# One layer of a hybrid attention trunk: memory queries and outputs on scaled float16, part of the ff1 row sums inside the MLP loop, and another order of the splits

## Chip, core and metric

The kernel runs on one core of one Trainium2 chip. The core has a matrix engine (TensorE, PE in the profile), VectorE (DVE), ScalarE (ACT), GpSimd (POOL) and the engine that issues most transfers (SyncE, SP). The metric is the device time of one execution in microseconds; 1422.9 us is the median of three runs of the kernel before (1422.52 to 1423.31).

## The reference

x is 1024 rows of 1024 numbers; everything is float32. One layer (the two attentions themselves are left out):

```python
h = rmsnorm(x, g_mix_pre)
proj = h @ w_in                     # q, k, v of 8 + 8 heads of 64, 8 forget logits
y = concat(rmsnorm(fox_attention, g_fox_out), rmsnorm(chunked_attention, g_chk_out))
x = x + rmsnorm(y @ w_out, g_mix_post)
h = rmsnorm(x, g_mem_pre)
mem_n = rmsnorm(mem, g_mem_kv)      # 256 memory rows
q = h @ w_mq                        # 4 heads of 256
p = softmax(q @ (mem_n @ w_mk).T / 16)
y = (p @ (mem_n @ w_mv)) @ w_mo
x = x + rmsnorm(y, g_mem_post)
h = rmsnorm(x, g_ff_pre)
y = square(relu(h @ w_ff1)) @ w_ff2 # 1024 -> 4096 -> 1024
x = x + rmsnorm(y, g_ff_post)
```

## The kernel before

Every float32 product is made of three matmuls on a high and a low part of each operand (`mm3`, L202 to L206: high*high, low*high, high*low; in the profile L204, L205, L206). The parts are either a rounded 32-bit form, or float16 after a scaling by a power of two that keeps them in range. Before the change, queries, keys, values of the first attention and the MLP are on scaled float16; the memory block is on the 32-bit form. A split is always ACT (copy or scaled copy to the high part) and then DVE or POOL (rest minus high part to the low part).

The program has three pieces. First the entry: norm of x, transposes, values. Then attention in eight pairs of heads, with the k and v of the memory behind it. Then a second phase: output projection (tiles `yw`), norm and transposes (`tr_h2T`), memory queries (`mq`, a Strassen product of seven half-size products), scores (`ms`), transposes of the probabilities (`mtr`), memory outputs (`mo`), and the output projection of the memory (`ym`, Strassen for rows 0 to 511, plain for the others). Last the MLP: a loop over j = 0 to 15, each a Strassen step on one 128-column block of each of the two halves of w_ff1 (products on PE in the order `px`, `py`, `px`, `pz`, `px`, `pv`, `pz`), then the second product (`fx`). The rows of w_ff1 that are meant by "rows" below are its 32 column blocks of 128.

Attention and second phase are ordered by a planner that runs when the program is built (`Flow`, L58). PE's work comes as streams of steps, each with a cost and a condition; the first stream whose condition holds gives the next step. Work of the other engines goes into queues for V (DVE), S (ACT), G (POOL) and D (transfers) by `put`, with an earliest time, a cost and a level; when an engine is free the item of the lowest level that is due is issued (`upto`, L95). `Tokens` (L41) count buffers. `Stock` (L413) loads and splits the weights in a fixed list; `Norms` (L1249) loads w_ff1 once more during attention, block by block, for the sums of squares (`wn`) from which the scale of all of w_ff1 is made (`sw1`, its inverse `us1`; both columns of `fsc`). `close_row` (L1411) ends a row block of a projection: root of the sum of squares, addition to x, store, square sum of the new x, root, scaling.

The MLP's order is written by hand. In iteration j, `nxt` is the block of j + 1 and `after` that of j + 2. `Weights` (L2577) holds the two raw slabs of a block (`wf`), their Strassen sums made by POOL (`sc`, `sd`, L2595 to L2602), and the splits: `whi_a`, `wlo_a` of the first slab, `v0hi_s` and so on of the sums. `nxt.split("a")` stands between the fourth and the fifth product of an iteration; the first two products of the next iteration read it. `relu2` (L2360) applies the inverse scale and squares. `first_row` (L2397) makes the first two products. Iterations up to `AHEAD` = 7 have part of their work done earlier. At j = 14 `second_scales` (L1315) makes the scale of w_ff2 and of the squared features.

## Time and profile before

| | |
|---|---|
| median of 3 runs | 1422.9 us |
| profiled execution | 1422.69 us |
| its span | 1420.7 us |
| granted PE clock over the span | 0.999 |
| busy: PE, DVE, ACT, POOL | 98%, 81%, 69%, 32% |

The span is from the first to the last instruction of the core; about 2 us of the device time lie outside it. A matmul's record is longer than its pitch, since consecutive matmuls overlap; where PE is gapless its time is the number of matmuls times the distance of their starts. Views are quoted as they print: a timeline row has start, duration, engine, line, operation, and in brackets the idle time before it and what ended that; a group's row has busy time, mean duration in ns, and the idle time before its members.

### The profile page before, as it was taken

What the parts mean: (1) busy time and instruction counts of PE and PEld (TensorE: products, weight loads), DVE (VectorE), ACT (ScalarE), POOL (GpSimd) and SP (SyncE); (2) the same over time, 40 slices, a digit from 0 to 9 for tenths busy, and PEclk for the clock granted to TensorE, in tenths of its full rate; (3) what the DMA queues carried; (4) which work ended last, traced back from release to release, by engine and by line L of the source; (5) the groups of instructions that cost most, each with busy time, mean ns of one, the idle gap of its engine ahead of it and who ended that gap; (6) DMA issues with size and microseconds to landing.
All of it is one profiled execution on the core that took longest, in us unless ns stands there. A gap on an engine that the chain in (4) does not pass through costs nothing.

```text
span 1420.7 us, 22525 instructions
## 1 busy us (share of the span) xinstructions
PE 1394.8 (98%) x7681; PEld 917.3 (65%) x7681; DVE 1152.9 (81%) x1863; ACT 987.1 (69%) x1688; POOL 452.6 (32%) x615
## 2 busy tenths in 40 slices
PE   8999999999999999999999999999999999999998
...
PEclk9999999999999999999999999999999999999999
...
DMA packets 118802, 295.72 MB, mean 208 GB/s; under 512 B 13448, under 2 KB 31888, under 8 KB 118688
## 3 DMA queue, kind: packets, MB, share of 16 engines
...
## 4 chain that ended last, share of the span: by engine, by line
PE 75%; DVE 10%; ACT 6%; issue 5%; DMA 2%; POOL 1%; SPq 0%; DVEq 0%; ACTq 0%; POOLq 0%
PE ptr L804 4%; PE fx L204 3%; PE fx L206 3%; PE fx L205 3%; PE px L206 2%; PE px L204 2%; PE px L205 2%; PE pv L849 2%; PE yw L204 2%; PE yw L205 2%; PE yw L206 2%; PE mq L205 2%; PE mq L206 2%; PE mq L204 2%; PE k L204 2%
## 5 line engine op out<-in xcount | busy, mean ns | idle before, releaser
L814 ACT ACTIVATE phl<-ptr 128x512 f16<-128x512 f32 (+3 forms) x152 | 79.5, 537 | 25.5 <-PE ptr L804 22.7
L2900 POOL TENSOR_SCALAR rf<-sf 128x1 f32<-128x1 f32 x7 | 5.8, 826 | 280.3 <-ACT jf L2879 280.0
L2595 POOL TENSOR_TENSOR sc<-wf,wf 128x512 f32<-128x512 f32 x8 | 11.2, 1396 | 172.4 <-DMA wf<-in_w_ff 122.8
L810 DVE SCALAR_TENSOR_TENSOR phl<-ptr,phl 128x384 f16<-128x384 f32 (+1 forms) x76 | 45.8, 616 | 14.5 <-ACT phl L814 14.1
L1746 POOL TENSOR_SCALAR mp<-mp,mst 128x256 f32<-128x256 f32 x32 | 21.3, 673 | 108.8 <-DVE mst L1745 102.1
L812 DVE TENSOR_TENSOR phl<-ptr,phl 128x384 fp32r<-128x384 f32 (+1 forms) x76 | 46.6, 617 | 8.5 <-ACT phl L814 7.8
L2744 ACT ACTIVATE vhif<-ra,fsc 128x1024 f16<-128x1024 f32 x34 | 38.9, 1144 | 21.1 <-PE fx L206 10.2
L849 PE MATMUL pv<-phl,vs 128*128 128x512 f32 (+1 forms) x152 | 52.8, 428 | 0.0
L2746 DVE SCALAR_TENSOR_TENSOR vhif<-ra,fsc,vhif 128x1024 f16<-128x1024 f32 x34 | 43.5, 1281 | 10.6 <-ACT vhif L2744 10.3
L2744 ACT ACTIVATE whif<-ra,fsc 128x1024 f16<-128x1024 f32 x34 | 38.9, 1143 | 18.8 <-PE fx L206 10.3
L204 PE MATMUL yw<-whiwo,yT_hi 128*128 128x512 f32 x128 | 50.8, 397 | 0.0
L205 PE MATMUL yw<-wlowo,yT_hi 128*128 128x512 f32 x128 | 50.2, 392 | 0.0
L206 PE MATMUL yw<-whiwo,yT_lo 128*128 128x512 f32 x128 | 50.1, 391 | 0.0
L204 PE MATMUL fx<-vlof,vhif 128*128 128x512 f16 x128 | 48.5, 379 | 0.8 <-DVE yc L2951 0.8
L204 PE MATMUL q<-hF_hi,wq 128*128 128x512 f16 x128 | 48.9, 382 | 0.2 <-DVE qs L953 0.2
L204 PE MATMUL k<-hF_hi,wk 128*128 128x512 f16 x128 | 49.0, 383 | 0.0
L2746 DVE SCALAR_TENSOR_TENSOR whif<-ra,fsc,whif 128x1024 f16<-128x1024 f32 x34 | 43.5, 1280 | 6.5 <-ACT whif L2744 6.4
L206 PE MATMUL q<-hF_hi,wq 128*128 128x512 f16 x128 | 48.5, 379 | 0.0
L204 PE MATMUL fx<-wlof,whif 128*128 128x512 f16 x128 | 48.5, 379 | 0.0
L205 PE MATMUL fx<-wlof,whif 128*128 128x512 f16 x128 | 48.5, 379 | 0.0
L206 PE MATMUL fx<-wlof,whif 128*128 128x512 f16 x128 | 48.5, 379 | 0.0
L205 PE MATMUL k<-hF_lo,wk 128*128 128x512 f16 x128 | 48.5, 379 | 0.0
...
## 6 DMA issues: line engine op xcount, KB each, us to landing
wg<-in_w_ff SPq DMA_DIRECT2D x48, 512.0 KB, 5.7
ra<-gd SPq DMA_DIRECT2D x40, 512.0 KB, 5.3
wf<-in_w_ff SPq DMA_DIRECT2D x38, 512.0 KB, 4.8
wn<-in_w_ff SPq DMA_DIRECT2D x32, 512.0 KB, 4.9
w2n<-in_w_ff SPq DMA_DIRECT2D x32, 512.0 KB, 6.0
wi<-in_w_ff2q SPq DMA_DIRECT2D x28, 512.0 KB, 5.5
...
```

The costliest lines, as they stand in the source:

```text
L204: nc.tensor.matmul(ps, lh, rh, start=start, stop=False, skip_group_check=more)
L205: nc.tensor.matmul(ps, lh, rl, start=False, stop=False, skip_group_check=more)
L206: nc.tensor.matmul(ps, ll, rh, start=False, stop=stop, skip_group_check=more)
L804: nc.tensor.transpose(tr[:, m, :], sp[:, k * P:(k + 1) * P], ident)
L810: flow.put("V", at, 0.75, lambda: nc.vector.scalar_tensor_tensor(pl[:, live, :], tr[:, live, :], 2.0 ** 14, ph[:, live, :], op0=ALU.mult, ...
L812: if ph.dtype == F16 else nc.vector.tensor_sub(pl[:, live, :], tr[:, live, :], f(ph[:, live, :])), done)
L814: flow.put("S", flow.end, 0.6, lambda ph=ph, tr=tr, live=live: nc.scalar.activation(ph[:, live, :], tr[:, live, :], AF.Copy, scale=2.0 ** ...
L849: nc.tensor.matmul(pv[:, :, qs_, :], v, hl[:, :, hs, :], start=c == 0 and turn == 0, stop=last)
L1746: mul = lambda st=st, pr=pr: nc.gpsimd.tensor_scalar(pr, pr, st[:, 2:3], 1.0, op0=ALU.mult, op1=ALU.mult)
L2595: eng.tensor_sub(sc[:, k1], r0[:, k0], r1[:, k0])
L2744: nc.scalar.activation(ah, ra, AF.Copy, scale=su)
L2746: nc.vector.scalar_tensor_tensor(al, ra, su, ah, op0=ALU.mult, op1=ALU.subtract)
```

## The change

It has four parts.

1. **Memory block on scaled float16.** The weights of `mq` and `mo`, the query operands and the outputs of the memory attention are split into float16 parts. Scales come from sums of squares: of 16 query blocks and 16 output blocks on ACT, the gain of the norm, and the memory values; each set goes through a small matmul (`mqn`, `mon`), DVE and POOL. `mq` splits wait for the condition "query scales", `mo` splits and the transposes of the probabilities for "output scales". Where two buffers of 32-bit parts were needed, one holds both float16 parts.
2. **Row sums in the MLP.** Attention squares only 14 of the 32 blocks of w_ff1 (`EARLY_ROWS`: those of j = 0 to 6). For j = 7 to 15 each block has its own scale: two ACT squares of the raw slabs at the end of iteration j - 2, two 128x1 matmuls (`nw`) behind the third product of iteration j - 1, a clip on DVE and four instructions on POOL, which give `rowsc` (scale, and its inverse for `relu2`). The splits of that block use `rowsc` in place of `fsc`. The scale of the squared features is then made at j = 14 (`feature_scale`), from all 32 sums.
3. **Row sums in the row's tile.** `close_row` adds x into the row's own tile, so that the tile of x is given back earlier; the last scaling of the mixer's rows is on POOL in place of ACT, and waits for the store of the row as well as for the root.
4. **Order.** Items of the planner may have a level that depends on how near their weights are to use (`rank`); chains may be strictly ordered (`Line`); most levels and costs have new numbers, some pools have more buffers, and the streams stand in another order. The high and low parts of the second half of x (`hF[1]`) are made by the planner in place of all before attention.

The core of the diff:

```diff
+    def late_half(kc, x):
+        eng = "G" if kc in LATE else "V"
+        hi = lambda: nc.scalar.activation(hF[1].hi(kc), x, AF.Copy)
+        lo = lambda: (nc.gpsimd if eng == "G" else nc.vector).tensor_sub(hF[1].lo(kc), x, hF[1].hi(kc))
+        flow.put("S", 0.0, 0.63, hi, lambda at: flow.put(
+            eng, at, 1.45 if eng == "G" else 1.15, lo, mark(("hF", kc)), 2), 2)
...
         for kc in range(KC):
-            x, e = xT[1][kc // 2][:, kc % 2, :], nc.gpsimd if kc in LATE else nc.vector
-            nc.scalar.activation(hF[1].hi(kc), x, AF.Copy)
-            e.tensor_sub(hF[1].lo(kc), x, hF[1].hi(kc))
+            late_half(kc, xT[1][kc // 2][:, kc % 2, :])
+        seen["k", 0], seen["sq", ("q", 1)] = 5.9, 0.5
         flow.free.update(BUSY)
         free["raw"].free = list(RAWS)
+        flow.put("S", 20.0, 0.4, lambda: nc.scalar.activation(gmsq, gmem, AF.Square, accum_out=fsm[:, 16:17]), None, 0)
         km, vmh, vml = attention_phase()
...
-            item = min(i for i in self.waiting[e] if i[1] <= start)
+            item = min((i for i in self.waiting[e] if i[1] <= start),
+                       key=lambda i: (i[0]() if callable(i[0]) else i[0], i[1], i[2]))
...
+        def rank(self, key, near, far):
+            return lambda: near if self.places[key] <= self.place + NEAR else far
...
+            if key[0] in ("mq", "mo"):
+                shape.insert(1, 2)
+                x = (u4(nm, shape, F16) if home == "u4" else
+                     (p2x if home == "wq" else wp).tile(shape, F16, tag=home, bufs=2, name=nm))
+                self.w[key] = x[:, 0], x[:, 1]
+                c = smq if key[0] == "mq" else smo
+                if eng == "G":
+                    return nc.gpsimd.tensor_scalar(x[:, 0], raw, c, 1.0, op0=ALU.mult, op1=ALU.mult)
+                return nc.scalar.activation(x[:, 0], raw, AF.Copy, scale=c)
...
+    EARLY_ROWS = [*range(7), *range(16, 23)]
...
+        def squares(self):
+
+            j, c = self.j, 2 * self.j
+            junk = pw.tile([P, D], BF16, tag="junk", bufs=1, name=f"jn{j}")
+            for k in range(2):
+                nc.scalar.activation(junk, self.raw[k], AF.Square, scale=1.0 / 32.0, accum_out=wsq[:, c + k:c + k + 1])
+
+        def scales(self):
+            c = 2 * self.j
+            ps = bank(f"nw{self.j}")
+            for k in range(2):
+                nc.tensor.matmul(ps[:, 0:1], o1024.to_broadcast([P, P]), wsq[:, c + k:c + k + 1], start=k == 0, stop=k == 1)
+            nc.vector.tensor_scalar(self.u, ps[:, 0:1], 2.0 ** -48, None, op0=ALU.max)
+            nc.gpsimd.tensor_tensor(self.scale, self.u, mhalf[:, 0:1], op=ALU.pow)
+            nc.gpsimd.tensor_tensor(self.u, self.u, phalf, op=ALU.pow)
+            nc.gpsimd.tensor_scalar(self.scale, self.scale, 8.0, 1.0, op0=ALU.mult, op1=ALU.mult)
+            nc.gpsimd.tensor_scalar(self.u, self.u, isx1, 0.125, op0=ALU.mult, op1=ALU.mult)
 
...
+            if more and j + 1 >= AHEAD:
+                nxt.scales()
...
-            relu2(g11)
+            relu2(g11, cur.u)
...
+            if after and after.j >= AHEAD:
+                after.squares()
...
             if j + 2 == NP:
+                feature_scale()
                 second_scales()
...
+    def feature_scale():
+
+        ps = mm_tile([P, 32], "norms1", "pv")
+        nc.tensor.matmul(ps, o1024.to_broadcast([P, P]), wsq[:, 0:32], start=True, stop=True)
+        nc.vector.tensor_reduce(su, ps, axis=mybir.AxisListType.X, op=ALU.max)
+        rsqrt(su, 1)
+        nc.vector.scalar_tensor_tensor(su, su, 2.0 ** -14, sr, op0=ALU.mult, op1=ALU.mult)
+        nc.vector.tensor_tensor(su, su, su, op=ALU.mult)
+        power_below(su)
...
-            rest = [("S", 1.1, lambda: square_sum(xin[nm, n], s2)),
-                    ("G", 1.5, lambda: root(1, s2)),
-                    ("S", 1.1, lambda: nc.scalar.activation(y, xin[nm, n], AF.Copy, scale=r[1])) if gnext == "mem" else
-                    ("V", 1.3, lambda: nc.vector.scalar_tensor_tensor(y, xin[nm, n], r[1], gains[gnext],
-                                                                      op0=ALU.mult, op1=ALU.mult))]
-            flow.chain(end, rest, lambda t_: (free[row_home[nm, n]].give(t_), then(t_)), 1)
+            if gnext == "mem" and n not in ROWS:
+                last = "S", 1.1, lambda: nc.scalar.activation(y, y, AF.Copy, scale=r[1])
+            elif gnext == "mem":
+                last = "G", 1.5, lambda: nc.gpsimd.tensor_scalar(y, y, r[1], 1.0, op0=ALU.mult, op1=ALU.mult)
+            else:
+                last = "V", 1.5, lambda: nc.vector.scalar_tensor_tensor(y, y, r[1], gains[gnext], op0=ALU.mult, op1=ALU.mult)
+            both = all_of(("row", nm, n), 2, lambda at: flow.put(last[0], at, last[1], last[2], then, 1))
+            flow.load(end, lambda: nc.sync.dma_start(dst[n], y), lambda at: (
+                seen.__setitem__(("x1d", n), at) if nm == "w" else None, both(at)), 3)
+            flow.chain(end, [("S", 1.1, lambda: square_sum(y, s2)),
...
-        flow.chain(at, [("S", 0.6, lambda: nc.scalar.activation(hi, c, AF.Copy, scale=0.0625)),
-                        ("V", 0.7, lambda: nc.vector.scalar_tensor_tensor(lo, c, 0.0625, f(hi), op0=ALU.mult, op1=ALU.subtract))],
-                   done, 0)
+        copy = lambda: nc.scalar.activation(hi, c, AF.Copy, scale=uq)
+        rest = lambda: nc.vector.scalar_tensor_tensor(lo, c, uq, f(hi), op0=ALU.mult, op1=ALU.subtract)
+        if order:
```

Where instructions now stand, in the rows of each engine's program (line, operation, outputs and inputs with buffer numbers, shape, and the engines or transfers that it waits for). First ACT around the head of iteration j = 9; `p_9` and `u_9` are copies of PE's products, `g_9` and `u_8` results under `relu2`. Before:

```order
L2361 ACTIVATE u_8_11556<-u_8_11556,fsc 128x512 [waits DVE_49]
L2362 ACTIVATE u_8_11556<-u_8_11556 128x512 [waits Activation_49]
L2404 ACTIVATE p_9_11667<-px_11641 128x512 [waits DMAHW5_49,PE_49]
L2785 ACTIVATE u_9_11683<-px_11641 128x512 [waits DMAHW7_49,PE_49]
L2361 ACTIVATE u_8_11505<-u_8_11505,fsc 128x512 [waits DVE_49]
L2362 ACTIVATE u_8_11505<-u_8_11505 128x512 [waits Activation_49]
L2361 ACTIVATE g_9_11669<-g_9_11669,fsc 128x512 [waits DMAHW6_49,DVE_49]
L2362 ACTIVATE g_9_11669<-g_9_11669 128x512 [waits Activation_49]
L2341 ACTIVATE whi_a_11714<-wf_11451,fsc 128x1024 [waits DMAHW3_49]
L2341 ACTIVATE v0hi_s_11718<-sc_11625,fsc 128x1024 [waits Pool_49]
L2803 ACTIVATE u_9_11734<-px_11641 128x512 [waits PE_49]
```

After:

```order
L2771 ACTIVATE jn_11635,wsq<-wf_11459 128x1024 [waits DMAHW1_49]
L2771 ACTIVATE jn_11635,wsq<-wf_11582 128x1024 [waits DMAHW7_49,Activation_49]
L2583 ACTIVATE p_9_11686<-px_11660 128x512 [waits DMAHW3_49,PE_49]
L2986 ACTIVATE u_9_11710<-px_11660 128x512 [waits DMAHW5_49,PE_49]
L2540 ACTIVATE u_8_11521<-u_8_11521,rowsc 128x512 [waits DVE_49]
L2541 ACTIVATE u_8_11521<-u_8_11521 128x512 [waits Activation_49]
L2540 ACTIVATE g_9_11688<-g_9_11688,rowsc 128x512 [waits DMAHW4_49,DVE_49,Pool_49]
L2541 ACTIVATE g_9_11688<-g_9_11688 128x512 [waits Activation_49]
L2520 ACTIVATE whi_a_11741<-wf_11459,rowsc 128x1024 [waits Pool_49]
L2520 ACTIVATE v0hi_s_11745<-sc_11644,rowsc 128x1024
L3004 ACTIVATE u_9_11761<-px_11660 128x512 [waits PE_49]
```

The two squares (`jn`) of the slabs of j = 10 stand ahead of `p_9`, and `whi_a` and `v0hi_s` use `rowsc`: `whi_a` now waits for POOL.

DVE from the addition that ends the second product of iteration 9. Before:

```order
L2406 TENSOR_TENSOR g_9_11669<-py_11654,p_9_11667 128x512 [waits DMAHW6_49,PE_49,Activation_49]
L2847 TENSOR_TENSOR s_8_11687<-u_8_11505,g_8_11558 128x512 [waits DMAHW2_49,Activation_49]
L2853 TENSOR_TENSOR u_8_11505<-g_8_11491,u_8_11505 128x512 [waits DVE_49]
L2855 TENSOR_TENSOR s_8_11690<-s_8_11687,g_8_11491 128x512 [waits DMAHW2_49]
L2857 TENSOR_TENSOR s_8_11691<-u_8_11556,s_8_11690 128x512 [waits DMAHW3_49,DVE_49]
L2344 SCALAR_TENSOR_TENSOR wlo_a_11715<-wf_11451,fsc,whi_a_11714 128x1024 [waits Activation_49]
L2344 SCALAR_TENSOR_TENSOR v0lo_s_11719<-sc_11625,fsc,v0hi_s_11718 128x1024 [waits Activation_49]
L2805 TENSOR_TENSOR g_9_11736<-pz_11701,u_9_11734 128x512 [waits DMAHW7_49,Activation_49]
```

After:

```order
L2585 TENSOR_TENSOR g_9_11688<-py_11673,p_9_11686 128x512 [waits DMAHW4_49,PE_49,Activation_49]
L2778 TENSOR_SCALAR rowsc<-nw_11702 128x1 [waits PE_49]
L3050 TENSOR_TENSOR s_8_11714<-u_8_11521,g_8_11574 128x512 [waits DMAHW0_49,Activation_49]
L3056 TENSOR_TENSOR u_8_11521<-g_8_11499,u_8_11521 128x512 [waits DVE_49]
L3058 TENSOR_TENSOR s_8_11717<-s_8_11714,g_8_11499 128x512 [waits DMAHW0_49]
L3060 TENSOR_TENSOR s_8_11718<-u_8_11572,s_8_11717 128x512 [waits DMAHW1_49,DVE_49]
L2523 SCALAR_TENSOR_TENSOR wlo_a_11742<-wf_11459,rowsc,whi_a_11741 128x1024 [waits Activation_49]
L2523 SCALAR_TENSOR_TENSOR v0lo_s_11746<-sc_11644,rowsc,v0hi_s_11745 128x1024 [waits Activation_49]
L3006 TENSOR_TENSOR g_9_11763<-pz_11728,u_9_11761 128x512 [waits DMAHW5_49,Activation_49]
```

The clip of `nw` is the second row; the additions behind it and the low parts are as before.

POOL in the same iteration, all that it does there, after; before it had the first four rows alone:

```order
L2794 TENSOR_TENSOR sc_11644<-wf_11459,wf_11582 128x512 [waits DMAHW7_49,DMAHW1_49,DVE_49]
L2795 TENSOR_TENSOR wf_11582<-wf_11582 128x512 [waits DMAHW2_49,DMAHW4_49,Activation_49,Pool_49]
L2796 TENSOR_TENSOR sc_11644<-wf_11582,wf_11459 128x512 [waits Pool_49]
L2801 TENSOR_TENSOR sd_11648<-wf_11459,sc_11644 128x512 [waits DVE_49,Pool_49]
L2779 TENSOR_TENSOR rowsc<-rowsc,mhalf 128x1 [waits DVE_49]
L2780 TENSOR_TENSOR rowsc<-rowsc,phalf 128x1 [waits Pool_49]
L2781 TENSOR_SCALAR rowsc<-rowsc 128x1
L2782 TENSOR_SCALAR rowsc<-rowsc,fsc 128x1 [waits Pool_49]
```

The first four rows are the Strassen sums of the next slabs, the others the chain of the scale; ACT's `whi_a` reads the scale that the last row but one writes.

PE at the start of attention: `nq` is the small matmul on the squares of the second k block. Before:

```order
L205 MATMUL k_0_925<-hF_lo_696,wk_728 128x512
L206 LDWEIGHTS wk_728
L206 MATMUL k_0_925<-hF_hi_694,wk_728 128x512
L481 MATMUL nq_940<-nq,o_83 128x1 [waits Activation_49]
L204 LDWEIGHTS wk_728
L204 MATMUL k_0_925<-hF_hi_694,wk_728 128x512
L205 LDWEIGHTS wk_728
L205 MATMUL k_0_925<-hF_lo_696,wk_728 128x512
```

After:

```order
L231 MATMUL q_1_976<-hF_lo_708,wq_734 128x512
L232 LDWEIGHTS wq_734
L232 MATMUL q_1_976<-hF_hi_706,wq_734 128x512
L519 MATMUL nq_986<-nq,o_83 128x1 [waits Activation_49]
L230 LDWEIGHTS wq_734
L230 MATMUL q_1_976<-hF_hi_706,wq_734 128x512
L231 LDWEIGHTS wq_734
L231 MATMUL q_1_976<-hF_lo_708,wq_734 128x512 [waits DVE_49]
```

It moved from within the first `k_0` into the second half of the first query product, 21 matmuls later. ACT ahead of the squares (`wk`, with the sum `nq`), before:

```order
L2255 ACTIVATE hF_hi_698<-xT_437 128x512 x2
L2255 ACTIVATE hF_hi_698<-xT_439 128x512 x2
L2255 ACTIVATE hF_hi_699<-xT_441 128x512 x2
L2255 ACTIVATE hF_hi_699<-xT_443 128x512 x2
L471 ACTIVATE wk_929,nq<-wrawk_888 128x1024 [waits DMAHW3_49]
L952 ACTIVATE qs_923<-q_0_892,wus 64x512 [waits PE_49]
L952 ACTIVATE qs_924<-q_0_892,wus 64x512
```

After:

```order
L2230 ACTIVATE hF_hi_706<-xT_444 128x512 x2
L1010 ACTIVATE qs_917<-q_0_883,wus 64x512 [waits PE_49]
L1010 ACTIVATE qs_918<-q_0_883,wus 64x512
L2230 ACTIVATE hF_hi_706<-xT_446 128x512 x2
L2230 ACTIVATE hF_hi_707<-xT_448 128x512 x2
L2230 ACTIVATE hF_hi_707<-xT_450 128x512 x2
L509 ACTIVATE wk_973,nq<-wrawk_881 128x1024 [waits DMAHW4_49]
L1017 ACTIVATE kd_969<-k_0_923,wus 64x512 [waits PE_49]
L1017 ACTIVATE kd_971<-k_0_923,wus 64x512
```

Two copies of the first query product (`qs`) now stand among the eight high parts (`hF_hi`), ahead of the squares. In the second phase the first transpose `tr_h2T` comes 27 matmuls later on PE than before.

459 lines of the change are left out of this document (287 added, 172 removed).

## The prediction, made before the changed kernel was run

> **What bounds the kernel now.** I read the page first: its totals, then the rows of forty slices.
>
> ```profile
> span 1420.7 us, 22525 instructions
> PE 1394.8 (98%) x7681; PEld 917.3 (65%) x7681; DVE 1152.9 (81%) x1863; ACT 987.1 (69%) x1688; POOL 452.6 (32%) x615
> PE   8999999999999999999999999999999999999998
> PEclk9999999999999999999999999999999999999999
> ```
>
> TensorE (PE) is busy 98% of the span, in every slice, at the full granted clock. It works in program order, so the time is the pitch of its matmuls plus the holes between them, and an edit counts only if it changes one of these two. So I then took PE's waits by releaser; the rows that matter here are:
>
> ```profile
> PE nq L481 <- ACT wk L471: 2.6, 2, 2.1
> PE ftr L613 <- DVE wsc L482: 0.6, 2, 0.4
> PE tr_h2T L1555 <- ACT yw L1434: 1.6, 1, 1.6
> PE ptr L804 <- POOL spc0g L747: 0.9, 1, 0.9
> PE pz L204 <- DVE g L2805: 0.7, 2, 0.5
> ```
>
> All holes that this view lists are a few us each. What the change can win is therefore pitch (its float16 part) and some of these holes; what it can lose is new holes.
>
> **Part 1: float16 in the memory block.** It changes the type of all `mq` and `ym` matmuls. The groups of `mq` have x16 each in 21 rows (336); `ym` has 21 rows of x8 in the Strassen half and three of x64 (360). Together 696.
>
> ```profile
> 810.00:828.00 18.00, 18.00 (x81) 1.00 0.67 223
> 1140.00:1158.00 18.00, 18.00 (x85) 1.00 0.95 334
> L205 PE MATMUL ym<-wlomo,oT_hi 128*128 128x512 f32 x64 | 24.9, 389 | 0.0
> L204 PE MATMUL ym<-whimo,oT_hi 128*128 128x512 f32 x64 | 25.4, 396 | 0.0
> L204 PE MATMUL fx<-vlof,vhif 128*128 128x512 f16 x128 | 48.5, 379 | 0.8 <-DVE yc L2951 0.8
> ```
>
> The first two rows are stretches of 18 us in which PE does nothing but 32-bit `ym`, and nothing but float16 `fx`: 81 against 85 matmuls, so 4.7% of the pitch, about 10.5 ns. By duration the difference is 10 (389) to 17 ns (396), 12.7 as the mean of the three `ym` rows (396, 390, 389) against 379. I take 12 ns: 696 x 0.012 = **-8.4 us**, with 10 and 14 ns as ends (-7.0, -9.7). Of this I give back 0.9: the rows from 815 on go through chains of DVE, POOL and ACT into the MLP's first operands, and these don't shorten.
>
> The same 12 ns from a rule: the Trainium skill, "TensorE: Matmul & The Clock Gate", section "Wait — 56ns, not 53.3ns?", has N/2.4 GHz + 2.5 ns from start to start, 215.7 ns for 512 columns, for warm back-to-back matmuls; the float16 stretch agrees (216 in a row), the 32-bit one does not (227). By the rule alone part 1 would bring nothing (rival D).
>
> **Part 2: row sums and scales of the last ff1 rows in the MLP.** Eighteen squares leave attention, where they cost PE nothing (all holes of PE between 100 and 560 us add up to about 1 us), and arrive in iterations j = 5 to 13. There each iteration gets two ACT squares, two tiny `nw` matmuls on PE, a DVE clip, four POOL instructions, and from j = 6 on the split of the next block's first slab (`whi_a`) waits for POOL's result. What that meets is seen in the rows of one iteration (j = 11, PE from 1040.42 to 1058.86), DVE, then ACT, then the chain's end on PE:
>
> ```profile
> 1049.90 0.68 DVE L2406 TENSOR_TENSOR g<-py,p 128x512 f32<-128x512 f32 x1
> 1050.50 0.68 DVE L2847 TENSOR_TENSOR s<-u,g 128x512 f32<-128x512 f32 x1
> 1051.21 0.69 DVE L2853 TENSOR_TENSOR u<-g,u 128x512 f32<-128x512 f32 x1
> 1051.82 0.68 DVE L2855 TENSOR_TENSOR s<-s,g 128x512 f32<-128x512 f32 x1
> 1053.15 1.28 DVE L2344 SCALAR_TENSOR_TENSOR wlo_a<-wf,fsc,whi_a 128x1024 f16<-128x1024 f32 x1
> 1054.35 1.28 DVE L2344 SCALAR_TENSOR_TENSOR v0lo_s<-sc,fsc,v0hi_s 128x1024 f16<-128x1024 f32 x1
> 1055.54 0.68 DVE L2805 TENSOR_TENSOR g<-pz,u 128x512 f32<-128x512 f32 x1
> 1051.91 1.13 ACT L2341 ACTIVATE whi_a<-wf,fsc 128x1024 f16<-128x1024 f32 x1
> 1056.17 0.06 DVE g L2805
> 1056.28 0.38 PE pz L204
> ```
>
> `whi_a` ends 1053.04, `wlo_a` follows at once, then `v0lo_s`, then the addition `g` (L2805), and PE's last product starts 0.06 us behind that: this chain has **no slack**, in all of iterations 8 to 14 (PE stands 0.1 to 0.7 us there each time). So every us by which the scale comes after the old start of `whi_a` is paid in full, once per iteration.
>
> When does the scale come? The clip is queued on DVE behind `g` (L2406, ends 1050.58); POOL then raises to a power twice and multiplies, and only then may ACT start. Prices of such 128x1 instructions:
>
> ```profile
> 1118.80 0.55 POOL L1278 TENSOR_TENSOR fsc<-fsc,mhalf 128x1 f32<-128x1 f32 x1 [15.99 <-DVE fsc L1277]
> 1399.98 0.84 POOL L2900 TENSOR_SCALAR rf<-sf 128x1 f32<-128x1 f32 x1
> 1400.90 0.91 POOL L2901 TENSOR_TENSOR rf<-rf,mhalf 128x1 f32<-128x1 f32 x1
> 1399.99 2.73 DVE L2924 SCALAR_TENSOR_TENSOR xf<-yc,rf,xf 128x512 f32<-128x512 f32 x4
> L1195 POOL TENSOR_SCALAR h3x<-s2h 128x1 f32<-128x1 f32 x3 | 0.7, 223 | 8.0 <-ACT junk L1190 8.0
> ```
>
> A power takes 0.55 alone and 0.91 beside back-to-back DVE additions of two SBUF tiles, a multiplication 0.22 alone and 0.84 beside them. Behind the clip DVE runs exactly such additions (L2847 to L2857, 0.7 us apart). Alone: 0.15 clip + 0.23 to POOL + 0.55 + 0.08 + 0.55 + 0.08 + 0.22 = 1.9 us after `g`; each slowed: 0.38 + 0.91 + 0.08 + 0.91 + 0.08 + 0.84 = 3.2. The first power starts in the middle of an addition, the later ones near an edge between two, so I take 2.65. The old gap from `g` to `whi_a` is 1.33 us (1050.58 to 1051.91) in j = 8, 9, 11 and 12; in 10 and 13 POOL's own weight sums end later than `g` and set the start, and `whi_a` would come 0.8 and 1.05 late; in 14 it is 1.1 and in 7 there are 4.9 us of room. That is 4 x 1.32 + 0.8 + 1.05 + 1.1 = 8.2 us; 3.5 with the chain alone (where a gap falls below the 0.4 us of `nw`, that counts), 12 with each instruction slowed.
>
> The Trainium skill, "SBUF — State Buffer", section "SBUF: two separate sides", says why: VectorE with two SBUF inputs and GpSimd share one port pair as an exclusive lock for a whole instruction. The rows around 1400 agree. By the rule at its worst the chain is that of rival B, 4.0 us, and this term 18 us.
>
> The other pieces. `nw`: a 128x1 32-bit matmul is two records of 0.1 us:
>
> ```profile
> 486.64 0.79 PE ssh L1176 x8
> ```
>
> So 0.4 us per iteration; inside the late ones it lies ahead of the hole and is hidden, in j = 6 and 7 it counts: +0.8. The squares are 2 x (1.04 + 0.19) of ACT, at the head of an iteration, where ACT idles (0.76 us before `p`, 4.58 behind it):
>
> ```profile
> 1043.21 0.60 ACT L2404 ACTIVATE p<-px 128x512 f32<-128x512 f32 x1 [0.76 <-PE px L206]
> 1048.39 0.60 ACT L2785 ACTIVATE u<-px 128x512 f32<-128x512 f32 x1 [4.58 <-PE px L206]
> L1247 ACT ACTIVATE w2n<-w2n 128x1024 f32<-128x1024 f32 x32 | 33.3, 1042 | 0.0
> ```
>
> `p` moves from 2.8 to about 4.4 us after the iteration's start and must free its bank by 5.2, so this hides; without that room it costs up to 0.4 per iteration, mostly where the second raw slab lands late. In j = 14 and 15 the scale of ff2 is now made behind one more reduction, power and five tiny DVE operations, 1.3 to 1.9 us ahead of the copy that frees PE's next bank: +1.4. **Sum of part 2: 8.2 + 0.8 + 1.4 = +10.4** (ends +6 and +15).
>
> **Part 3: the order of attention and of the second phase.** At 67.84 PE waits for the squares of the second k block, because ACT first makes eight halves of `hF_hi`:
>
> ```profile
> 62.47 4.28 ACT L2255 ACTIVATE hF_hi<-xT 128x512 f16<-128x512 f32 x8
> 66.63 1.07 ACT L471 ACTIVATE wk<-wrawk 128x1024 f16<-128x1024 f32 x1
> 67.84 0.38 PE L481 MATMUL nq<-nq,o 128*128 128x1 f32 x2 [2.13 <-ACT wk L471]
> ```
>
> Now this `nq` stands 21 matmuls (4.8 us) later on PE, while on ACT only two copies (1.4 us) come ahead of the squares: the 2.1 us go. The holes behind it belong to the same late start (the rows of waits above: 2.6 at `nq` in all, 0.6 at `ftr`, 0.9 at `ptr`, together 4.1), so I take -4.0; next late would be `ftr`, which follows `nq` on PE at once. Ends -5 and 0. In the second phase the first `tr_h2T` comes 27 matmuls (6 us) later, so its 1.6 us go; the gates on the new scales can add holes. Each row of the mixer is now scaled only when its store has landed, which takes 2.9 us:
>
> ```profile
> x1d<-xtw SPq DMA_DIRECT2D x8, 512.0 KB, 2.9
> ```
>
> against 2.3 for the square sum and power beside it: 0.6 later, inside the 6 us. -1.5, ends -4 and +6. The rest (three small matmuls, a multiplication on POOL): +0.3.
>
> **Sum.** 1422.7 (span 1420.7 plus 2) - 8.4 + 0.9 + 10.4 - 4.0 - 1.5 + 0.3 = 1420.4; the profiled execution is 0.2 below the median, so **1420.6**.
>
> **Rivals.** A, *the scale is in time*: DVE reaches `g` earlier, since POOL's sums, which slow its additions, now wait for the squares. It decides if `g` comes 1.3 us earlier; then part 2 costs 0.8 + 1.4 + what is left, some 3 us, and the time is 1413 (1408 to 1417). For it: `g` stands at 6.1 to 10.5 us in the iteration, so it does move with its neighbours; against it: the slowed additions come as many as before. B, *slower: POOL's chain under DVE*: each of POOL's three instructions waits for a whole addition (0.69, L2853), 1.9 + 2.1 = 4.0 us, so `whi_a` comes 2.7 us late in four iterations and 2.1 to 2.4 in three, 18 + 2.2 instead of 10.4: 1430 (1426 to 1435). It decides from 3.4 us on; the rows of 0.84 and 0.91 bear it out, that the later two start near an edge speaks against it. C, *the planner's new gates starve PE*: `mq` and `ym` splits wait for scales that need all 16 square sums and stored sums; one gate late by the 6 us of the end above and no win at the start give 1432 (1424 to 1434). Against it: the second phase now has only 4 us of holes. D, *float16 does not shorten the stretch*, since other engines feed it or the pitch stays: 8.4 - 0.9 more, 1428; the 85 against 81 speak against it.
>
> **How the numbers follow.** Forecast (1416 to 1425.5): 0.52, a little under half of it below 1420.05; A 0.20; B 0.12; C 0.11; D 0.05. About 0.2% (2.8 us) is what a measurement of this kernel can tell from no change. Faster: 0.25 + 0.20 = 0.45. Same (1420.05 to 1425.75): 0.27 + 0.02 of C + 0.01 of D = 0.30. Slower: 0.12 + 0.09 + 0.04 = 0.25. The range 1410 to 1431 leaves out the better end of A (0.06) and the worse ends of B and C (0.10).
>
> **What would show it.** Part 1: the `mq` and `ym` groups at 379 ns, stretches of 18 us with 83 to 85 matmuls. Part 2: `whi_a` released by POOL, a hole of about 1.3 us on PE before the last `pz` of iterations 8 to 14, and no hole before `px`; without those holes it is A, with holes over 2 us B. Part 3: no wait of `nq` on `wk`, none of `tr_h2T` on `yw`; new waits with `query scales` or `output scales` behind them mean C. The forecast is wrong if the holes between 100 and 560 us, now 1 us, exceed 4.

## The result, and the profile after

The changed kernel takes 1440.1 us (1437.6 to 1441.6), the kernel before 1422.7 beside it: ratio 1.0121, interval 1.0103 to 1.0138. That is 17.4 us slower, where 1420.6 was forecast with 1431 as the upper end. The page of the changed kernel: its totals, then the rows of forty slices.

```profile
span 1437.9 us, 22721 instructions
...
PE 1396.7 (97%) x7723; PEld 868.3 (60%) x7723; DVE 1167.1 (81%) x1886; ACT 1011.6 (70%) x1750; POOL 534.4 (37%) x679
...
PE   9989999999999999979999999999999999999998
...
PEclk9999999999999999989999999999999999999999
```

Two slices of PE are no longer full, the third and the eighteenth, and in the eighteenth PEclk, the granted clock, falls to 8 tenths. Before, PE stood at 9 in all slices but the first and the last, and PEclk in all. PE's waits by releaser (us in total, times, longest) show new names:

```profile
PE tr_h2T L1707 <- POOL yw L1570: 10.2, 2, 6.4
PE k L230 <- DVE qs L1011: 3.5, 1, 3.5
...
PE sf1g L786 <- DVE mnf0g L790: 2.0, 1, 2.0
PE py L230 <- DVE fsc L1384: 2.0, 1, 2.0
PE trx L2654 <- DVE ym L2710: 2.0, 1, 2.0
...
PE pz L230 <- DVE g L3006: 1.2, 2, 1.0
```

`nq <- wk` is gone, as forecast; in its place come `k`, `sf1g`, `trx`, `py` and above all `tr_h2T`. To see what these cost I split PE's time in each trace. For every form of matmul I took the median distance from one start to the next; the matmuls times these medians are the *work*, and whatever a distance has above its median is *excess*, put where it stands.

| | before | after | with float16 alone (e17) |
|---|---|---|---|
| work | 1382.3 | 1373.7 | 1371.6 |
| excess 0 to 80 us | 9.8 | 5.8 | 10.8 |
| 80 to 200 | 4.4 | 8.6 | 3.2 |
| 200 to 575 | 2.4 | 9.5 | 3.6 |
| 575 to 660 | 4.3 | 13.5 | 5.3 |
| 660 to 880 | 3.2 | 9.1 | 7.2 |
| 880 to 1165 | 5.0 | 8.1 | 4.9 |
| from 1165 | 0.9 | 0.9 | 1.2 |

Work fell by 8.6, excess rose by 25.5: together 16.9 of the span's 17.2. The medians are each trace's own. That of the 32-bit matmuls of 512 columns is 231 ns before and 228 after; 784 of these are left, so 2.4 us stand under excess that would be work at 231 ns (then work falls by 6.2, excess rises by 23.1, and the second phase stays the largest piece). Windows of the second phase (us, then busy time and count for PE, PEld, DVE, ACT, POOL, then PEclk, DMA share, GB/s), and PE's own rows there (start, duration, what ended the idle time):

```profile
600.00:610.00 10.00, 10.00 (x54) 8.52 (x53) 9.27 (x15) 9.42 (x26) 4.53 (x4) 1.00 0.98 354
610.00:620.00 10.00, 1.67 (x7) 0.83 (x5) 8.84 (x12) 8.83 (x13) 8.43 (x6) 0.68 0.81 287
620.00:630.00 10.00, 8.12 (x33) 5.27 (x34) 6.63 (x6) 4.86 (x11) 3.34 (x2) 0.63 0.39 150
```

```profile
604.49 1.91 PE L1707 MATMUL tr_h2T<-ident,yw 128*128 128x128 f32 x16
...
610.80 0.39 PE L232 MATMUL yw<-whiwo,yT_lo 128*128 128x512 f32 x1
617.64 0.48 PE L1707 MATMUL tr_h2T<-ident,yw 128*128 128x128 f32 x1 [6.45 <-POOL yw L1570]
621.88 3.46 PE L1707 MATMUL tr_h2T<-ident,yw 128*128 128x128 f32 x15 [3.77 <-POOL yw L1570]
625.14 0.63 PE L230 MATMUL mq<-A11q,mq_B 128*128 128x512 f16 x1
...
627.52 0.38 PE L230 MATMUL mq<-A11q,mq_B 128*128 128x512 f16 x1
```

The second group of transposes (604.49) finds its rows ready. The third stands straight behind the last `yw` and waits for two rows that POOL must still scale. In the kernel before, 60 matmuls of `mq` lie between the two, and the third group waits for nothing:

```profile
607.35 0.39 PE L206 MATMUL yw<-whiwo,yT_lo 128*128 128x512 f32 x1
607.58 0.39 PE L204 MATMUL mq<-A11q_h,whimq_B 128*128 128x512 f32 x1
...
622.30 1.91 PE L1555 MATMUL tr_h2T<-ident,yw 128*128 128x128 f32 x16
```

The other thing to see is what happens *after* the wait: 15 transposes take 3.46 us, where 16 took 1.91, and the first `mq` take 0.63 instead of 0.38. PE was granted half its clock from 613.7 to 627.3. Apart from the run's end there are four more such stretches, at 94.9 (6.8 us), 207.5, 839.0 and 1132.5 (3.4 each), each right behind a hole of about 2 us or more. In the kernel before there is none until the last 2 us of its span.

### The profile page after: what moved, and what is told of

It is laid out like the page before. It is cut to its first block, busy times and chain, and to the rows that moved or that the text cites. A ratio compares the mean times of both kernels' runs of the same rounds, so it can differ in the third digit from the quotient of the medians.

```text
span 1437.9 us, 22721 instructions
## 1 busy us (share of the span) xinstructions
PE 1396.7 (97%) x7723; PEld 868.3 (60%) x7723; DVE 1167.1 (81%) x1886; ACT 1011.6 (70%) x1750; POOL 534.4 (37%) x679
## 5 line engine op out<-in xcount | busy, mean ns | idle before, releaser
L1910 POOL TENSOR_SCALAR mp<-mp,mst 128x256 f32<-128x256 f32 x32 | 29.4, 930 | 116.3 <-DVE mst L1909 111.5
L2943 ACT ACTIVATE vhif<-ra,fsc 128x1024 f16<-128x1024 f32 x34 | 38.9, 1143 | 20.7 <-PE fx L232 10.2
L230 PE MATMUL k<-hF_hi,wk 128*128 128x512 f16 x128 | 49.6, 387 | 3.5 <-DVE qs L1011 3.5
L232 PE MATMUL k<-hF_hi,wk 128*128 128x512 f16 x128 | 49.3, 385 | 0.0
L231 PE MATMUL q<-hF_lo,wq 128*128 128x512 f16 x128 | 48.8, 381 | 0.0
L230 PE MATMUL fx<-wlof,whif 128*128 128x512 f16 x128 | 48.5, 379 | 0.0
L231 PE MATMUL fx<-wlof,whif 128*128 128x512 f16 x128 | 48.5, 379 | 0.0
```

Of the source, the lines that this page charges most:

```text
L230: nc.tensor.matmul(ps, lh, rh, start=start, stop=False, skip_group_check=more)
L231: nc.tensor.matmul(ps, lh, rl, start=False, stop=False, skip_group_check=more)
L232: nc.tensor.matmul(ps, ll, rh, start=False, stop=stop, skip_group_check=more)
L1910: mul = lambda st=st, pr=pr: nc.gpsimd.tensor_scalar(pr, pr, st[:, 2:3], 1.0, op0=ALU.mult, op1=ALU.mult)
L2943: nc.scalar.activation(ah, ra, AF.Copy, scale=su)
```

## The experiments

All times are medians; the changed kernel is 1440.1. "Hole" is a wait of PE. A trace is one execution of four or five, up to 3 us off the median. The intervals of e2, e3, e6, e7, e9 and e11 to e14 overlap that of the changed kernel (1.0103 to 1.0138), so by their times alone these runs can't be told from it; what they show is read from their traces. e1, e5 and e15 stand clear of it, e16 all but clear; e8 and e17 change the kernel before, and stand clear of that one.

### Whose fault is the hole in the second phase: POOL, ACT or DVE?

POOL's rows in the changed kernel ahead of the third group:

```profile
612.12 0.93 POOL L1559 TENSOR_TENSOR rw<-rw,mhalf 128x1 f32<-128x1 f32 x1 [1.42 <-DVE rw L1554]
613.04 3.02 POOL L1648 TENSOR_SCALAR g_ff_pre<-g_ff_pre,fsc 128x1024 f32<-128x1024 f32 x1
616.04 1.55 POOL L1570 TENSOR_SCALAR yw<-yw,rw 128x1024 f32<-128x1024 f32 x1
617.55 1.51 POOL L1559 TENSOR_TENSOR rw<-rw,mhalf 128x1 f32<-128x1 f32 x1
619.05 2.77 POOL L1570 TENSOR_SCALAR yw<-yw,rw 128x1024 f32<-128x1024 f32 x1
```

The scaling of a gain (`g_ff_pre`, which nothing reads before 791 us) stands ahead of the two rows. So the first theory was POOL's order, and the first four runs here try to clear POOL's way.

**e1: rows scaled by ACT, with a new plan.**
```diff
-    ROWS = range(8)
+    ROWS = range(0)
```


> One edit to the changed kernel: the last scaling of the mixer's rows goes back from POOL to ACT (it still waits for the store). Theory 1: the two holes ahead of tr_h2T (6.4 and 3.8 us) come from POOL's queue, where a gain of 3.0 us and a row scaling slowed to 2.8 us stand ahead, and the half clock of 610 to 630 us comes from these holes: both holes fall below 1.5 us in sum, no half clock there, and the time falls by 9 to 13 us (to 1427 to 1431). Rival: the rows are late because their stores and additions are late; then ACT is released as late, the holes stay above 7 us and the time falls by less than 3 us.

Measured: 1459.0 (ratio 1.0251, 1.0228 to 1.0273). Neither theory came near. The planner makes another order when an operation changes its engine, and ACT is then late all through the second phase:

```profile
PE ms L230 <- ACT mp L1907: 6.8, 7, 1.4
PE tr_h2T L1707 <- ACT yw L1568: 6.4, 2, 3.7
```

**e2: the gain with the lowest urgency.**
```diff
-  gains[key], gains[key], sx if key == "ff" else um, ...), mark(key), 2)
+  gains[key], gains[key], sx if key == "ff" else um, ...), mark(key), 5)
```


> One number of the changed kernel: the level of the scaling of the gain g_ff_pre on POOL from 2 to 5, so that rows go first. Theory 1: the 3.0 us of that instruction leave the first hole; the holes ahead of tr_h2T go from 10.2 to about 7 us, the time falls by 3 to 4 us. Rival (the store or the addition releases the row): the row starts no earlier, the holes change by less than 1 us.

Measured: 1441.7 (1.0131, 1.0116 to 1.0146), the same holes of 6.44 and 3.77. When the planner filled POOL's slot nothing else was waiting there, so urgency decided nothing: the instructions of this run stand in the changed kernel's order on every engine, and the 1.6 us between the two medians come from measuring one order twice. From here on most edits keep the planner's slots and change only what is issued in them.

**e6: the gain issued in the slot of the other gain, all else in place.**
```diff
+  def scale():
+      for k, c in (("ff", sx), ("memo", um)) if key == "memo" else ():
+          nc.gpsimd.tensor_scalar(gains[k], gains[k], c, 1.0, ...)
```


> The changed kernel with one POOL instruction elsewhere: the 3.0 us scaling of g_ff_pre is issued beside that of g_mem_post, the order of all other instructions on all engines is kept. Theory 1 (the rows stand behind POOL's own queue): the two holes ahead of tr_h2T go from 10.2 to about 7 us, time -3 to -5 us with what the clock gives back. Rival (POOL has slack there, the row's input is late): no change within 1 us.

Measured: 1439.8 (1.0116, 1.0100 to 1.0133). Holes 4.92 and 3.45, 8.4 instead of 10.2: without the gain the row scalings themselves take 3.02 and 2.84 us beside DVE's additions.

**e7: the rows scaled by ACT, in the same slots.**
```diff
-  last = "G", 1.5, lambda: nc.gpsimd.tensor_scalar(y, y, r[1], 1.0, ...)
+  last = "G", 1.5, lambda: nc.scalar.activation(y, y, AF.Copy, scale=r[1])
```


> The changed kernel, the eight row scalings issued on ACT at the places that they had, no other instruction moved (run e1_rows_act let the planner order everything anew). Theory 1: tr_h2T's holes fall from 10.2 to 2 to 4 us, the half clock at 614 to 627 us shrinks to one stretch or none, time -8 to -12 us. Rival (ACT is as full as POOL there, as in e1_rows_act): holes above 6 us, time within 4 us of the changed kernel.

Measured: 1439.4 (1.0112, 1.0095 to 1.0130). Holes 5.36 and 2.46, 7.8 in all; on ACT the rows wait behind the splits of `mq_B` and `mq_T`. It was not POOL alone.

**e12: DVE relieved.** The low halves of the first five weight blocks of `mq` are left out; DVE copies the high half in their place.
```diff
+  return eng.tensor_copy(lo, hi) if key in [b[0] for b in self.blocks if b[0][0] == "mq"][:5] else ...
```


> Left out: the low halves of the first five mq weight blocks, which are replaced by a float16 copy of the high half (DVE, much shorter than 1.3 to 2.1 us); the order of all engines is unchanged. Theory (DVE, busy 90% between 560 and 620 us, makes the rows 4 and 5 late, directly and by slowing POOL): some 6 us of DVE go, POOL's gain and row scalings fall from 3.0, 1.55 and 2.8 to 1.1 to 1.6 each, the waits of tr_h2T fall from 10.2 to 6 to 7, A11q and A12q are ready 3 us earlier: 1435.5 (1434 to 1437). Rival (ACT's square sums and the order of PE set it): waits of tr_h2T stay above 9, 1439 to 1440.

Measured: 1438.3 (1.0112, 1.0097 to 1.0127). POOL's rows in this run:

```profile
611.55 1.11 POOL L1648 TENSOR_SCALAR g_ff_pre<-g_ff_pre,fsc 128x1024 f32<-128x1024 f32 x1
612.64 1.28 POOL L1570 TENSOR_SCALAR yw<-yw,rw 128x1024 f32<-128x1024 f32 x1
...
614.86 3.11 POOL L1570 TENSOR_SCALAR yw<-yw,rw 128x1024 f32<-128x1024 f32 x1
```

The gain fell from 3.02 to 1.11 us, the first row from 1.55 to 1.28; the second row now meets the subtractions of `A11q` and takes 3.11. Holes 7.8: DVE does slow POOL, and that is worth 2.4 us here, where I expected 3 to 4.

**e13: 24 matmuls of `mq` ahead of the third group.**
```diff
-  yield (0.436, lambda: there(*(("h2", ...
+  yield (0.436, lambda: (th == 0 or acc.get("n", 0) >= 8) and there(*(("h2", ...
```
(`acc["n"]` counts the steps of `mq`, three matmuls each)

> Changed: the third group of tr_h2T stands behind the first 24 matmuls of mq on PE instead of ahead of all 54; the planner fits the other engines to it (small differences). Theory (before, mq covered the rows' way; the order on PE took that cover away): PE waits for the low parts of A11q instead, which end at 619.8 (first) in the trace of the changed kernel, one hole of 8.6 us; the 16 transposes (1.75 us) then find their rows ready: mq 5.2 us earlier less 1.75, so -3.5: 1436.5 (1435 to 1438). Rival (the operands of mq are late for the same reason as the rows, DVE being full): the hole stays at 10 or more, 1439 to 1441.

Measured: 1439.1 (1.0120, 1.0105 to 1.0135). The transposes are now free of any wait, but `mq` waits for its own operands:

```profile
613.68 0.58 PE L230 MATMUL mq<-A11q,mq_B 128*128 128x512 f16 x1 [4.88 <-ACT A11q L1786]
617.45 0.58 PE L231 MATMUL mq<-A11q,mq_B 128*128 128x512 f16 x1 [3.19 <-DVE A11q L1788]
...
625.25 1.91 PE L1707 MATMUL tr_h2T<-ident,yw 128*128 128x128 f32 x16
```

A hole of 8.1, as the theory had it (8.6). But 14 matmuls behind it ran at half rate (0.427 us apart), against six of `mq` in the changed kernel, which took 1.7 of the expected 3.5 us. So behind the last `yw` three chains (rows by POOL, rows by ACT in e7, operands of `mq`) end 9 to 11 us later, and no single edit of these closes the hole. The operands come late because the new splits of the weights stand ahead of them. The two parts of `A11q` in the changed kernel, then in the kernel before:

```profile
614.98 1.99 ACT L1786 ACTIVATE A11q<-h2r 128x1024 f16<-128x1024 f32 x2
618.57 2.35 DVE L1788 TENSOR_TENSOR A11q<-h2r,A11q 128x1024 f16<-128x1024 f32 x2
```

```profile
603.07 2.06 ACT L1633 ACTIVATE A11q_h<-h2r 128x1024 fp32r<-128x1024 f32 x2
605.66 2.35 DVE L1635 TENSOR_TENSOR A11q_l<-h2r,A11q_h 128x1024 fp32r<-128x1024 f32 x2
```

In the changed kernel ACT makes three high halves of `mq_B` and `mq_T` (611.25 to 614.47) first, and DVE their low halves (up to 618.65). What the three chains share is DVE. One window of each kernel, before first (columns as above):

```profile
560.00:610.00 50.00, 48.35 (x232) 39.97 (x231) 38.58 (x60) 39.86 (x80) 8.99 (x12) 1.00 0.63 223
```

```profile
560.00:610.00 50.00, 49.20 (x239) 41.04 (x240) 46.22 (x73) 33.44 (x76) 25.00 (x21) 1.00 0.68 235
```

DVE does 46.2 us of work in 50 instead of 38.6, POOL 25.0 instead of 9.0, and ACT less. That DVE's load as a whole is the cause is argued from these rows; e12 shows 2.4 us of it. Of the load two pieces can be named. Eight sums of the weights of `mo` (`B11r` to `B22r`, 7.3 us), which were all done by 558 us before, now wait for ACT's new squares of the same weights and fall into this window. And in e7, with the rows off POOL and DVE's order as it was, DVE needs 43.1 us there (72 instructions) instead of 46.2 (73). What either costs PE no run shows by itself.

### Does a hole cost more than its length?

**e8: dead copies on ACT in the kernel *before*.** One to four of them stand ahead of `whi_a` in four iterations.
```diff
+  for _ in range({8: 1, 10: 2, 12: 3, 14: 4}.get(j, 0)):
+      nc.scalar.activation(idle, nxt.raw[0], AF.Copy)
```


> The kernel before, with 1, 2, 3 and 4 dead ACT copies of 1.04 us ahead of whi_a in iterations 8, 10, 12 and 14 (their results are not used). It measures two things by themselves: the slack of the chain whi_a to pz, and what a hole of a given length costs. My step in the prediction (no slack) says: holes of about 1.0, 2.0, 3.1 and 4.1 us at the last pz of these iterations, some 10 us in sum. Theory 4 (the clock): holes of 2 us and more are followed by a stretch of 3.4 us at half the clock, which costs another 1.7 us each: +15 us in all; the hole of 1 us is not. Rival: the holes cost their own length only, +10 us, and the half clock in the changed kernel has another cause.

Measured: 1435.7 (1.0090, 1.0075 to 1.0105), 13.1 more. The waits:

```profile
PE pz L204 <- DVE g L2808: 10.0, 4, 3.8
```

Four holes of 1.39, 2.08, 2.74 and 3.83 us, for copies of 1.0, 2.1, 3.2 and 4.3: the first hole has 0.5 us that was there before, and the last two are 0.5 shorter than their copies, so the chain has next to no slack. The rest goes with the clock: behind the third hole it is halved for 3.4 us, behind the fourth for 6.8, behind the first two not at all, which costs 1.6 and 2.8 us of slower matmuls in the trace. (Two more stretches, at 11 and 69 us, lie outside the edit.)

**e11: the wait filled with useless transposes.** 92 transposes of the unit matrix go into the bank that the third group overwrites.
```diff
+  [nc.tensor.transpose(tr[:, n % 2, n // 2 % 2, :], ident, ident) for n in range(92 * ((th, a, k) == (1, 0, 0)))]
```


> Added: 92 transposes of the constant unit matrix on PE ahead of the third group of tr_h2T, into the bank that this group overwrites; nothing waits for them. Theory (a PE that stands still gets the half clock in a later stretch): at 0.109 us each they fill the wait from 611.2 to about 621.2, so the listed waits of tr_h2T fall from 10.2 to about 1, no half-rate stretch begins near 614, the first mq starts at 623.7 instead of 625.1 and 8 of them take 0.216 instead of 0.427: 1437 (1435.5 to 1438.5). Rival (the half rate comes from what the chip does, not from the wait): the stretch at 613 to 627 stays slow, the added transposes take twice as long (20 us), and the time is 1447 or more. Second rival: what follows (A12q's low parts, ending at 624) is late next and takes the gain back: 1440.

Measured: 1438.6 (1.0113, 1.0098 to 1.0128). The window and the rows of PE:

```profile
610.00:620.00 10.00, 9.46 (x88) 9.22 (x85) 10.00 (x9) 6.71 (x9) 9.67 (x5) 1.00 0.78 275
```

```profile
608.87 10.21 PE L1704 MATMUL tr_h2T<-ident 128*128 128x128 f32 x92
...
619.73 1.86 PE L1707 MATMUL tr_h2T<-ident,yw 128*128 128x128 f32 x15 [0.54 <-POOL yw L1570]
621.42 0.38 PE L230 MATMUL mq<-A11q,mq_B 128*128 128x512 f16 x1
```

The rows come as late as ever, yet the clock stays at 1.00 and 15 transposes take 1.86 us instead of 3.46. The half rate comes from PE standing still. The excess from 575 to 660 falls from 13.5 to 0.9, against 10.2 us of added work: 2.4 us won in the trace. The median fell by 1.5.

### The start of attention

**e14: three instructions of the forget gates one place later on DVE.**
```diff
-  ("V", 1.2, lambda: nc.vector.tensor_sub(e, e, l)),
-  ("V", 1.3, lambda: nc.vector.scalar_tensor_tensor(e, z, 0.0, e, ...)),
-  ("V", 0.9, lambda: nc.vector.memset(u, 0.0)),
+  ("V", 1.2, lambda: None),
+  ("V", 1.3, lambda: nc.vector.tensor_sub(e, e, l)),
+  ("V", 0.9, lambda: nc.vector.scalar_tensor_tensor(e, z, 0.0, e, ...)),
```
(the memset then goes with the scan that follows)

> Changed: three DVE instructions of the forget gates at 89 to 95 us (L681, L682, and the memset of L683) each stand one place later on DVE, behind a low half of qs; nothing else moves. Theory (k at 94.0 waits because the gates, now urgent, go ahead of the low halves of qs): the low half that ended at 93.96 ends at 92.2, set by ACT's high half (ends 91.5): hole 3.5 becomes 1.7, the half-rate stretch at 94.9 shrinks from 6.8 to at most 3.4: -2 to -3.5, 1437.5. Rival (late next: ACT's halves or POOL's part take it): the hole keeps more than 2.8 us or moves to the next k; within 1 us of 1440.

Measured: 1438.1 (1.0105, 1.0088 to 1.0122). The hole at `k` is 1.77 instead of 3.49 and the half-rate stretch behind it is gone: excess from 80 to 200 us 5.2 instead of 8.6. The gates, now the most urgent work on DVE, had pushed ahead of the low halves of `qs`, whose bank `k` needs.

### What do the row scales in the MLP cost?

**e16: one scale for all rows.**
```diff
-  self.scale, self.u = (sw1, us1) if j < AHEAD else (rowsc[:, k, j:j + 1] for k in range(2))
+  self.scale, self.u = sw1, us1
-      nxt.scales()
-      after.squares()
+      nc.gpsimd.memset(wsq[:, 2 * after.j:2 * after.j + 2], 1.0)
```


> Left out: the row scales of the last 18 ff1 rows (their squares, nw matmuls, clips and POOL's four instructions; their columns of the sums are set to one by POOL, and all rows use the scale of the first 14). All that stands ahead of the MLP is as in the changed kernel. Theory (the scale was late in j = 8 and 9 only, the rest is nw): the loop goes back to 18.25 per iteration, -3 to -4.5: 1436.5 (1435.5 to 1437.5). Rival (the forecast's part 2, a late scale in seven iterations): -9 to -10, 1430.5.

Measured: 1435.0 (1.0093, 1.0078 to 1.0108), 5.1 less. From the start of iteration 6 to the end this trace falls 3.9 us further behind the kernel before, the changed kernel 8.2: the scales by themselves cost 4.3. Why so little? Chosen rows of DVE, POOL and ACT in iteration 11 of the changed kernel (it starts at 1052.88):

```profile
1060.72 0.68 DVE L2585 TENSOR_TENSOR g<-py,p 128x512 f32<-128x512 f32 x1
1061.32 0.14 DVE L2778 TENSOR_SCALAR rowsc<-nw 128x1 f32<-128x1 f32 x1
1061.90 0.54 POOL L2779 TENSOR_TENSOR rowsc<-rowsc,mhalf 128x1 f32<-128x1 f32 x1
1062.52 0.55 POOL L2780 TENSOR_TENSOR rowsc<-rowsc,phalf 128x1 f32<-128x1 f32 x1
1063.16 0.34 POOL L2781 TENSOR_SCALAR rowsc<-rowsc 128x1 f32<-128x1 f32 x1
1063.90 1.13 ACT L2520 ACTIVATE whi_a<-wf,rowsc 128x1024 f16<-128x1024 f32 x1
```

`g` ends 8.5 us after the iteration's start (10.2 before), the chain on POOL ends 2.1 us behind it, and `whi_a` starts at 11.0 after the start, where it started at 11.5 before. Only in j = 8 (10.6 and 12.7) and 9 (9.9 and 12.0) is it late.

**e9: why `g` comes early.** The second square reads the first slab again in every other iteration, so that ACT and then POOL need not wait for the second slab.
```diff
-  nc.scalar.activation(junk, self.raw[k], AF.Square, ...)
+  nc.scalar.activation(junk, self.raw[0 if j % 2 else k], AF.Square, ...)
```


> The changed kernel; in iterations ahead of an odd block (8, 10, 12, 14) the second square reads the first slab again (so the row sum of the second slab is left out there), and POOL's in-place sum of the second slab no longer waits for ACT. Theory 5: the pause of POOL (1.9 us at that wait) is why DVE reaches g early: in those iterations g ends 1 to 2 us later (as in the kernel before, 9 to 10 us), whi_a waits for the scale and holes of 0.5 to 1.3 us come back at pz, time +2 to +5 us. Rival: g is early because the slabs land earlier; then g and the time stay within 1 us.

Measured: 1440.3 (1.0128, 1.0111 to 1.0145). In j = 10 and 12 `g` ends 1.2 us later, 9.99 instead of 8.80 and 9.40 instead of 8.16 after the start, but only j = 10 gets longer (19.00 instead of 18.49); in j = 8 and 14, which have the edit too, `g` ends where it did, within 0.2 us. POOL's pause is part of why `g` is early; it has little left to decide.

**e5: all 32 sums in attention again.**
```diff
-    EARLY_ROWS = [*range(7), *range(16, 23)]
+    EARLY_ROWS = list(range(32))
```


> Part 2 undone in the changed kernel: all 32 ff1 blocks are squared in attention, one scale for all, no nw matmuls, no squares and no POOL chain in the MLP; the feature scale stays at j = 14. Theory 3: iterations 8 to 14 go back from 18.49 to 18.25 us and the two late ones (19.63, 18.91) lose their holes, together -3.8 us in the MLP; attention has room on ACT, so the rest stays within 2 us: time -2 to -6 us. Rival: the 18 squares and loads in attention make new holes there as large as what the MLP gains: time within 2 us of the changed kernel or slower.

Measured: 1469.8 (1.0322, 1.0304 to 1.0339). With the new order the squares don't fit in front; they end up in the second phase, on ACT:

```profile
PE ms L230 <- ACT mp L1907: 14.4, 11, 2.0
PE tr_h2T L1707 <- POOL yw L1570: 6.0, 1, 6.0
```

**e3: the feature scale ahead of the sums in j = 14.**
```diff
-                puts = [call() for call in later_sums[:1 + j % 2]]
-                del later_sums[:1 + j % 2]
-            if j + 2 == NP:
-                feature_scale()
+            if j + 2 == NP:
+                feature_scale()
+            if j >= AHEAD:
+                puts = ...
```


> One edit to the changed kernel: at j = 14 the matmul, the reduction and the scale of the squared features stand ahead of the last sums on DVE (eight additions of 0.42 us) in place of behind them. Theory 2: the 2.0 us hole at py waits for that reduction, and the half clock of 3.4 us behind it follows from the hole; both go: -3.3 to -3.9 us. Rival: the chain behind (power, five small DVE operations) holds the next bank, so that a hole of 1 to 2 us comes at the next product and the time falls by less than 1.5 us.

Measured: 1439.9 (1.0119, 1.0103 to 1.0134). The hole at `py` shrinks from 1.96 to 0.65 us and the half rate behind it is gone (excess 3.6 to 1.8 there), but in this run two holes of 0.95 and 0.80 us at 968 drew a half-rate stretch of their own, and the median is only 0.2 lower.

### Do the gains add up, and what is float16 worth alone?

**e15: e14, e3 and e13 together, and 74 transposes of the unit matrix ahead of the first `mq`.**
```diff
+  [nc.tensor.transpose(ps[:, n % 4 * P:n % 4 * P + P], ident, ident) for n in range(74 * ("n" not in acc))]
```


> Together: the gates one place later on DVE, the feature scale ahead of the sums in j = 14, the third group of tr_h2T behind 24 matmuls of mq, and 74 transposes of the constant unit matrix on PE ahead of the first mq, into the bank that mq overwrites. Theory (holes of PE and the half rate behind them are the whole loss, and they add up): against the changed kernel the gates give 1.7 of hole and about 1.7 of clock, the feature scale 1.8, the second phase 4.6 (first mq 617.5 at full rate, the transposes hidden): 1431 (1428 to 1434). Rival (each gain is used up by the next late operand, as three of the four single edits gave 1 to 2 us): 1436 or more, with new holes of PE behind 625 us that the single edits don't show.

Measured: 1433.8 (1.0073, 1.0056 to 1.0090), 6.4 less. The page's rows are full again:

```profile
PE   9989999999999999999999999999999999999998
...
PEclk9999999999999999999999999999999999999999
```

That is the slow end of the theory's range (1428 to 1434): most of the gains add up. Excess from 575 to 660 is 2.2 (and 8.1 of added transposes), but 200 to 575 keeps 10.3 and 660 to 880 keeps 9.1: small holes at `sf1g`, `ssh`, `yw`, `trx`, with the clock behind some, and iteration 6 has a half-rate stretch as in e3.

**e17: float16 alone, in the kernel before.** The weights of `mq` and `mo` are multiplied by a fixed 256; there are no sums of squares, no computed scales, and every instruction keeps its place.
```diff
+  dt, wide = (F16, [P, 2] + shape[1:]) if key[0] in ("mq", "mo") else (F32R, shape)
-  nc.scalar.activation(w[0], raw, AF.Copy)
+  nc.scalar.activation(w[0], raw, AF.Copy, scale=256.0 if dt == F16 else 1.0)
+  if key[0] in ("mq", "mo"):
+      return eng.scalar_tensor_tensor(lo, raw, 256.0, hi, op0=ALU.mult, op1=ALU.subtract)
```
(the forms of the queries and of the memory output become float16 pairs likewise)

> The kernel before with float16 high and low parts for mq and ym alone: the weights times a fixed 256 (taken out again at the queries; behind the memory output only the norm's EPS weighs 65536 times less), no sums, no scales, no new order, all instructions in their places. Theory (float16 is worth what the changed kernel's trace shows, 5.0 for mq and 5.4 for ym by the pitch of 231 and 216 ns, and the rest of the change loses it): 1413 (1411 to 1415). Rival (the shorter products let the second phase starve, since ACT, DVE and POOL have as much to do as before): new holes at tr_h2T, ms or ym of 4 us and more, 1418 to 1424.

Measured: **1416.0 (1415.5 to 1417.9), ratio 0.9955, 0.9941 to 0.9968**, faster than both kernels, though above the 1415 at the end of the expected range. The fixed factor suits weights of this size only; the changed kernel computes its scales from the data. By the end of `ym` this kernel is 7.5 us ahead of the kernel before. Then PE waits 2.0 us for `whi_a`, which ACT starts 5.7 us earlier than before and not 7.5, and runs at half rate behind it:

```profile
842.74 0.39 PE L206 MATMUL px<-h3T_hi,whi_a 128*128 128x512 f16 x1 [2.00 <-ACT whi_a L2347]
842.97 0.38 PE L207 MATMUL px<-h3T_lo,whi_a 128*128 128x512 f16 x1
...
844.89 0.63 PE L207 MATMUL px<-h3T_lo,whi_a 128*128 128x512 f16 x1
```

## Why the prediction was wrong, step by step

**Part 1, float16: right in mechanism and nearly in size.** I took 12 ns per matmul, -8.4. Where `mq` and `ym` run without a hole (starts less than 300 ns apart), their starts are 230 and 229 ns apart on average before, and 216 after and in e17: some 13 ns, -9.2, inside my ends. (The medians behind the table's work, 231 to 216 ns, make it 15 ns and -10.4; but 231 is the median over all 32-bit matmuls of 512 columns, and that of `ym` alone is 227.) The group now stands at the 379 ns of other float16 products:

```profile
L230 PE MATMUL ym<-mo,oT 128*128 128x512 f16 x64 | 24.3, 379 | 0.3 <-DVE h3T_lo L1677 0.3
```

Rival D (no shorter stretch) fell. "I give back 0.9" was too small: e17 loses 2.0 at the named place and some clock behind it.

**Part 2, the row scales: mechanism right in two iterations, and a sum that came near by luck.** I had 8.2 for a late scale in seven iterations, 0.8 for `nw` and 1.4 for the feature scale: 10.4. From iteration 6 to the end the changed kernel lost 8.2, but not by these terms. The late scale cost some 1.5, `nw` included: j = 8 and 9 took 19.63 and 18.91 us instead of 18.80 and 18.25. The others mostly took 18.49 instead of 18.25 (`nw`, in nearly all of them and not only in j = 6 and 7), and j = 6 took 1.5 more, where `nw` also waits 0.8 for ACT's squares. Up to the start of j = 15 that is 4.5. `g` comes earlier, by 1.6 us in j = 11, which is rival A's reason, and POOL's chain takes 2.1 us, not 2.65. e8 confirms the step "no slack" to within 0.5 us, e16 the size (4.3 by the traces, 5.1 by the medians). The feature scale was the other way: 3.8 instead of 1.4, a hole of 2.0 and the clock behind it. Rival B (POOL in DVE's shadow, 4.0 us) did not happen here.

**Part 3, the order: here the prediction failed.** At the start I had -4.0, and the excess up to 80 us fell by just that, 9.8 to 5.8. That it fits so well is luck: the named holes at `nq` and `ftr` make 2.7 of it, `ptr` waits as long as before (1.1 us at 98), and 0.8 is a hole at `v` near 10 us that this trace lacks and others of the same order have (1.4 in e2). And the step "next late would be `ftr`" was wrong: next late were the low halves of `qs`, behind the gates, and 4.2 came back between 80 and 200 us (e14). In the second phase the step was "the first `tr_h2T` comes 27 matmuls later, so its 1.6 us go", and the later rows "inside the 6 us". For the first two groups that holds; they have no hole. I did not look at the third. Before, 60 matmuls of `mq` stood on PE between the last `yw` and that group. Now it follows the last `yw` at once, with nothing else for PE to do, because the operands of `mq` come later too (e13). So -1.5 became +9.2. Rival C named the phase and a size of that kind, but not the cause: the query scale was ready at 422 us and the output scale at 590, and what came late were the splits and row scalings queued behind on full engines.

**What the prediction had no term for: the clock.** I priced every hole at its length. The five half-rate stretches cost about 10 us in slower matmuls: 2.5 at 95 us (a hole of 1.1 lies inside), some 2.7 behind `tr_h2T`, where part of the stretch is the hole itself, and 1.6 at each of the three others. e8 shows it in the kernel before, e11 that filling the wait prevents it. My own test for failure, holes of more than 4 us between 100 and 560, was not met (2.8 us); the large holes lay at 94 and 618. Still, the excess from 200 to 575 rose by 7.1 and that from 660 to 880 by 5.9, for which I had nothing: holes of about 2 us at `sf1g` and `trx`, 0.8 at `ssh` and at `yw`, and the clock behind the first two.

What stays open: what each of the two named pieces of DVE's load between 560 and 610 us costs, and why `sf1g` and `trx` now wait; no run takes these up by themselves. Runs that moved an operation in the planner (e1, e5) got another order altogether and can't tell.
